# A two-layer decoder step on one core: eighteen entries of a table that delays steps of the woven work

## The chip, the cores and the metric

The kernel runs on one core of a Trainium2 chip. The metric is the device time of one execution in microseconds (us). The core has a matrix engine (PE, with PEld for its weight loads), a vector engine (DVE), a scalar engine (ACT), a general engine (POOL) and a queue that issues the DMAs (SP). Each of them works through its own instructions in the order in which the program gives them; they wait for one another by semaphores. PE writes only to PSUM, which the kernel divides into eight banks.

## The reference

One step of a decoder trunk with two layers, all in f32, for a prompt of 1024 tokens and for eight samples of four tokens each (32 rows). The width is 1024. Each layer computes

```
x <- x + gate(c) * Branch(RMSNorm(x) * (1 + scale(c)) + shift(c))
```

and a last RMSNorm follows. Layer 0's branch is sliding-window attention (16 query heads, 4 key heads of 64, a window of 128, a learned sink); for the samples it reads a cache of 128 keys and values. Layer 1's branch is a gated delta rule (8 key heads, 16 value heads of 128) after a causal convolution over four tokens:

```
def step(S, xs):
    w_v_c, w_k_c, qk_c, q_dec_c, k_dec_c, g_tot_c = xs
    u = w_v_c - w_k_c @ S
    o = q_dec_c @ S + qk_c @ u
    S = S * g_tot_c + k_dec_c.T @ u
```

For the prompt this recurrence runs in chunks, after a triangular solve in each chunk. For the samples each of 8 x 16 states of 128 x 128 is read from memory, used, updated and written back. Both branches end with a SiLU gate and an output projection. Besides the results for prompt and samples the kernel returns the new caches and states.

## The kernel before, in words

**Matrix work.** An f32 operand is split into a high and a low part (`hhi`, `hlo`, `wh`, `wl`), and each product is three matmuls (high by high, low by high, high by low). The bulk of PE's work is such products: the input projections of both layers (`project`, into the tiles `ps_pj`), then the output projections, in `out_block`, a block of 128 rows and two halves of 512 columns at a time. Layer 1 has 18 output blocks: heads 0 to 7 for eight blocks of rows and the samples, then heads 8 to 15 for seven blocks, the samples and the last block.

**The rest is woven in.** Everything else is written as generators, the jobs, which yield a condition wherever they would have to wait. After each matmul of a projection the builder calls `stages()`, which runs every job as far as its conditions let it. `Core.issued` keeps a model of when each engine will be free, so `ready(x)` says whether x should be there by the time at which PE has got, `idle(engine, x)` whether the engine is also free, `soon(x)` the same with some lead, and `bank(tag)` whether a PSUM bank is free; banks of one tag are handed on in turn. All this happens when the program is built: its outcome is the fixed order of the instructions in each engine's queue. `K` and `KR` rank the jobs where several could run.

**The table.** `LATE` (line 271) holds delays. Its key is the job's name, the how-manieth job of that name it is (from 0), and the number of yields that the job has passed. When the condition ahead of that step first holds, the step is held until the model's PE time has advanced by the entry's value, a number in us of that model. `held_off` (line 533) does this and `stages` (line 542) asks it:

```
def held_off(e):
    d = LATE.get((e[2], e[4], e[5]))
    if d is None or plain():
        return False
    if e[6] is None:
        e[6] = nc.free["tensor"]
    return nc.free["tensor"] < e[6] + d

def stages():
    ran = False
    for e in list(jobs):
        while e[0]() and not held_off(e):
            ran = True
            e[0] = next(e[1], None)
            e[5:7] = e[5] + 1, None
...
```

A held step holds back the rest of its own job, and other jobs go ahead of it. It makes no engine wait: an instruction that comes later in its queue still runs as soon as it is at the head and its operands are there. DMAs are the exception in the order: engines get the order of the program, while the DMA queue's order is arranged once more by the framework that places the instructions.

**The jobs that the change touches.**
- `attend_block` (line 1030), 32 of them in layer 0, a row block n for a pair of heads: scores into a bank `lg`, masked row maxima on DVE (`prob`, `mx`), four exponentials on ACT, sums and four scalings on DVE, transposes into banks `mi`, a copy on ACT and one on DVE (`pT`), and for every second block the product with the values into the bank `ob`. Blocks 0 to 15 read the keys of the first head pair; `kproj` (line 916) overwrites them for the second, once block 15 has issued its scores: its `evac` splits the new keys into `khh` (ACT) and `kll` (DVE) and so frees the projection's bank.
- `decayed` (line 2119), one for each key head in layer 1: k.q products for all chunks, eight to a group, multiplied into the decay tiles `DP` on DVE. `chain` (line 2142) is the recurrence over eight chunks; the key projection two heads on waits until a chain is through. `turn` (line 1897) transposes values. `gating` (line 2149) normalizes two chunks' output: sums on ACT, a reciprocal root on POOL, four scalings on ACT, transposes, a multiplication on DVE into `zl`, a store to `gTd`.
- `states_times` (line 2527), the job "states": 64 pieces of the samples' states (tiles `S`, four buffers) are loaded, two at a time multiplied on PE with keys and queries (into the bank `lg`), and the two buffers are loaded anew. It is paced by the progress of the output blocks.
- `core` (line 2580): the samples' recurrence. Its first step closes pools and issues four loads:

```
qk = flat(t2("qk2")).rearrange("p (i h t) -> p i h t", i=2, h=HQ)
nc.sync.dma_start(qk.rearrange("p i h t -> p (i h) t"), smd[0:2 * HQ].rearrange("n p t -> p n t"))
vs = t2("vs")
...
nc.sync.dma_start(gH, gbr[0].rearrange("h (b t) -> (h b) t", t=DS))
nc.sync.dma_start(bH, gbr[1].rearrange("h (b t) -> (h b) t", t=DS))
```

  It starts when chains, outputs and gatings are through (line 2583). Then it transposes on PE into banks `lg`, of which the states' job holds one until its last product, computes decays and 4 x 4 coefficients on DVE, waits for the states (line 2685), forms `VH` (the u), `U` and `oH` (the output) on DVE, and ends with `gsT`. The samples' output blocks (`prepare`, line 2349) wait for the whole core.
- `new_states` (line 2774), the job "new": from the moment the core has `U`, it loads the states once more, multiplies `kb` (ACT) with `U` on PE into banks `mi`, and updates `S` on DVE, two instructions to a product, then stores.
- `gather` (line 2423), one for each half block of the output (36): `y` on DVE from the bank, added to the row block `xt` on POOL (the very last on DVE), then squares on ACT. A gather starts when the one before it has added. `finish` (line 2396) scales a finished block and stores it. `prepare`, odd numbers from 3 on, is `rows_of` (line 2382), the load of a block of rows.

Of the kernel before, what the change touches and what calls it, by code (L numbers as in the profile page):

```python
# [226 lines left out]
def body(tc, I, O, cst_ap, dbg=None):  # L227
# [40 lines left out]
             ("z", 3), ("z", 4), ("z", 5), ("z", 6), ("z", 7)]  # L268
    SE = ("vector", "vector", "vector", "vector")
    LB_, SL = TB  # L270
    LATE = {('ahead', 13, 4): 0.4, ('ahead', 31, 4): 0.8, ('ahead', 57, 2): 0.8, ('attend', 10, 14): 4, ('attend', 12, 32): 1.5, ('attend', 13, 16): 1.5, ('attend', 20, 20): 0.8, ('attend', 22, 17): 0.8, ('attend', 4, 31): 0.4, ('attend', 9, 22): 0.4, ('blocks', 14, 9): 0.4, ('blocks', 5, 4): 0.6, ('blocks', 5, 5): 0.4, ('blocks', 9, 14): 2.5, ('cached', 0, 1): 0.4, ('cached', 1, 4): 0.6, ('cached', 1, 9): 0.4, ('cached', 3, 12): 0.8, ('cached', 3, 18): 0.4, ('cached', 3, 19): 0.8, ('cached', 4, 19): 0.8, ('cached', 4, 8): 2.5, ('chain', 0, 43): 1.3, ('chain', 1, 3): 1.4, ('chain', 2, 3): 2.7, ('chain', 6, 37): 0.4, ('chain', 6, 64): 1.5, ('chain', 7, 13): 0.4, ('chain', 7, 17): 0.4, ('core', 0, 70): 5, ('decay', 1, 6): 4, ('decay', 3, 16): 0.8, ('decayed', 2, 35): 1.5, ('decayed', 4, 25): 0.8, ('decays', 0, 26): 1.5, ('decays', 0, 29): 2.5, ('decays', 0, 43): 1.6, ('gather', 4, 2): 1.5, ('gating', 19, 11): 2.5, ('gating', 6, 11): 0.8, ('gating', 7, 2): 2.5, ('invert', 0, 23): 2.3, ('invert', 2, 22): 4, ('load', 0, 17): 1.5, ('load', 0, 38): 2.5, ('load', 0, 41): 0.4, ('mod', 0, 0): 1.5, ('mods', 0, 60): 2.3, ('mods', 0, 61): 1.5, ('new', 0, 60): 5.2, ('new', 0, 71): 0.7, ('new', 0, 93): 1.4, ('prepare', 0, 3): 3, ('prepare', 0, 8): 0.8, ('prepare', 8, 3): 2.5, ('rows', 0, 2): 1.5, ('samples', 11, 3): 1, ('samples', 18, 3): 1.2, ('samples', 2, 3): 1.5, ('samples', 26, 7): 0.4, ('shape', 7, 12): 0.7, ('shape', 8, 5): 1.5, ('shapes', 0, 21): 4, ('solve', 3, 23): 1.5, ('solve', 3, 7): 0.4, ('split', 0, 3): 0.4, ('split', 0, 6): 2.5, ('split', 3, 1): 1.5, ('squares', 0, 2): 1.5, ('states', 0, 51): 1.5, ('taps', 0, 2): 0.4, ('taps', 3, 2): 4.8, ('taps', 32, 2): 2.5, ('taps', 37, 2): 0.8, ('taps', 4, 2): 4, ('taps', 58, 3): 2.5, ('taps', 6, 3): 1.5, ('taps', 7, 2): 0.8, ('taps', 9, 1): 2.5, ('taps', 94, 2): 0.8, ('turn', 18, 4): 1.7, ('turn', 25, 4): 0.9, ('turn', 26, 4): 2.9}
    XB, FB, ZK, HK0, HK1 = 13, 3, 5, 7, 3

    def psb(tag=None):
# [53 lines left out]
    rows = xp.tile([64, P], F32, name="rows")  # L328
# [84 lines left out]
    def modulation_gate(l, gw, nw, tag):  # L413

        for j in range(2):
            c0 = 2 * D + 512 * j
            nc.sync.dma_start(modGt[32 * j:32 * j + 32], I["b_mod"][l:l + 1, c0:c0 + 512].partition_broadcast(32))
        pg = psb("lg" if l == 0 else "tr")
        wts = {}

        def load(m):

            wts[m] = []
            for k in (2 * m, 2 * m + 1):
                for j in range(2):
                    wt = gw.tile([P, 512], F32, tag=tag, name="wmod", bufs=nw)
                    nc.sync.dma_start(wt, I["w_mod"][l, k * P:(k + 1) * P, 2 * D + j * 512:2 * D + (j + 1) * 512])
                    wts[m].append(wt)

        def step(m):  # L430
            for q, wt in enumerate(wts.pop(m)):
                mm = nc.tensor.matmul(pg[32 * q:32 * q + 32, :], cT[:, 2 * m + q // 2, :], wt, start=(m == 0),
                                      stop=(m == KD // 2 - 1), skip_group_check=True)
            pin[:] = [mm]

        def end():
            nc.vector.tensor_tensor(modGt[0:64], modGt[0:64], pg[0:64, :], ALU.add)
            nc.scalar.copy(modGt[64:P], pg[64:P, :])

        if l == 0:  # L440
            return load, step, end

        def steps():
            load(0)
            for m in range(KD // 2):
                yield lambda: pos[0] >= MS[0] + MS[1] * (2 * m + 1)
                yield ready(*wts[m])
                step(m)
                if m + 1 < KD // 2:
                    load(m + 1)  # L450
            yield soon(pg)
            yield idle("vector", modGt)
            end()

        return steps()
# [77 lines left out]
# [4 lines that stand above are left out]
# [27 lines left out]
    def plain():  # L564
        return not isinstance(nc, Core)
# [311 lines left out]
    if True:  # L877
# [461 lines left out]
        load, step, end = modulation_gate(0, at, 8, "wg")  # L1339
# [441 lines left out]
    if True:  # L1781
# [518 lines left out]
        states = {0: {}}  # L2300
# [571 lines left out]
```

## Time and profile before

| | |
|---|---|
| three runs | 1663.89 us (median), 1662.79 to 1664.79 |
| the profiled execution | 1657.81 us |
| its span, first to last instruction | 1656.0 us |
| PE busy | 1577.5 us of the span |
| DVE, ACT, POOL busy | 1212.5, 871.7, 567.9 us |
| granted PE clock, mean | 0.987 |

The profile is taken from one execution, which has its own time. Rows of the timeline read: start, duration, engine, line, operation, output <- inputs, shapes, how many were merged, and in brackets how long the engine was idle before it and what ended that. Nearly all instructions have line 90, that of the wrapper `Engine` that records them, so a group is known by its tiles. SPq is the DMA queue's issuing, the DMA itself lands later. Names are given without their numbers: `S` stands for `S0` of the states' job, for `S1` of the new states and for the chains' `S`; `qk` for the core's `qk2` too.

### The profile page before, as it was taken

To read this page: it belongs to the slowest core of one execution; us is meant where nothing else is said; L and a number is where in the kernel's file an instruction comes from. 1 tells how busy PE (TensorE), PEld (TensorE's weight loads), DVE (VectorE), ACT (ScalarE), POOL (GpSimd) and SP (SyncE) were. 2 spreads that over 40 slices of the span, in tenths; PEclk is the share of its full clock that TensorE was granted. 3 is DMA by queue.
4 is the path that set the end of the run, shared out by engine and by line. 5 is a ranking of instruction groups with operands and counts; after the bars stand their busy time and mean duration, and the time that the engine had idled before them with its cause. 6 is when DMAs were issued, how large, how long until landed. Compare 5 with 4: busy or idle time off the path is not lost. (4 is left out here: it accounts for less than half of the span.)

```text
span 1656.0 us, 31448 instructions
## 1 busy us (share of the span) xinstructions
PE 1577.5 (95%) x10570; PEld 1333.3 (81%) x10570; DVE 1212.5 (73%) x3535; ACT 871.7 (53%) x2535; POOL 567.9 (34%) x1034
## 2 busy tenths in 40 slices
PE   6999999998999999999899999999999999998996
PEld 5787878887777888889888888988888886676784
DVE  6526767565666679898888778888798876367777
ACT  6535556444345637476473664655656654342332
POOL 1210101112223234363452433545245364333432
PEclk9999999999999999999999999999999999999998
DMA  9642211215344332233322323224132238773976
GB/s 319 184 140 72 67 44 52 65 36 147 115 140 117 94 86 51 69 102 80 99 62 79 89 63 110 54 77 123 47 108 69 57 95 237 232 219 113 281 237 201
DMA packets 286035, 191.76 MB, mean 116 GB/s; under 512 B 98601, under 2 KB 260393, under 8 KB 285842
## 3 DMA queue, kind: packets, MB, share of 16 engines
q1 hardware_dynamic: 285874, 189.75, 40.0%
q8 instruction: 84, 1.38, 0.3%
q14 instruction: 77, 0.63, 0.1%
HBM read 144.68 MB, written 47.04 MB: 116 GB/s over the span
## 5 line engine op out<-in xcount | busy, mean ns | idle before, releaser
L90 PE MATMUL ps_pj<-h2hi,wh 128*128 128x512 f32 (+2 forms) x1128 | 380.7, 337 | 1.4 <-ACT XR L90 1.4
L90 PE MATMUL ps_pj<-h2lo,wh 128*128 128x512 f32 (+2 forms) x1128 | 380.1, 337 | 0.0
L90 PE MATMUL ps_pj<-h2hi,wl 128*128 128x512 f32 (+2 forms) x1128 | 376.8, 334 | 0.0
L90 POOL TENSOR_TENSOR wl<-wr,wh 128x512 fp32r<-128x512 f32 x128 | 172.0, 1345 | 581.7 <-ACT wh L90 559.7
L90 PEld LDWEIGHTS ps_pj<-h2hi,wh 128*128 128x128 f32 x1128 | 213.9, 190 | 17.0 <-ACT XR L90 1.6
L90 PEld LDWEIGHTS ps_pj<-h2hi,wl 128*128 128x128 f32 x1128 | 214.2, 190 | 15.2 <-POOL wl L90 0.6
L90 PEld LDWEIGHTS ps_pj<-h2lo,wh 128*128 128x128 f32 x1128 | 214.2, 190 | 14.5
L90 PE MATMUL ps_pj<-hhi,wh 128*128 128x256 f32 (+2 forms) x376 | 122.4, 329 | 2.5 <-DVE kll L90 1.5
L90 PE MATMUL ps_pj<-hlo,wh 128*128 128x256 f32 (+2 forms) x376 | 122.8, 330 | 0.0
L90 PE MATMUL ps_pj<-hhi,wl 128*128 128x256 f32 (+2 forms) x376 | 121.9, 328 | 0.0
L90 POOL TENSOR_TENSOR xt<-xt,y 128x512 f32<-128x512 f32 (+1 forms) x47 | 63.9, 1365 | 165.4 <-DVE y L90 112.3
L90 DVE SCALAR_TENSOR_TENSOR vT<-XR,cT,vT 128x256 f32<-128x256 f32 (+1 forms) x144 | 85.5, 609 | 29.4 <-ACT vT L90 28.0
L90 DVE TENSOR_TENSOR tmp<-X 64x31 f32<-64x31 f32 (+15 forms) x248 | 95.2, 384 | 10.6 <-POOL X L90 6.9
L90 DVE TENSOR_TENSOR X<-X,tmp 64x31 f32<-64x31 f32 (+15 forms) x248 | 88.4, 356 | 8.5
L90 ACT CAST wh<-wr 128x512 fp32r<-128x512 f32 x128 | 78.6, 615 | 20.0 <-PE ps_pj L90 11.8
L90 PEld LDWEIGHTS ps_pj<-hlo,wh 128*128 128x128 f32 x376 | 70.4, 188 | 13.1 <-issue 8.7
L90 PEld LDWEIGHTS ps_pj<-hhi,wh 128*128 128x128 f32 x376 | 70.3, 188 | 10.6 <-issue 3.1
L90 PEld LDWEIGHTS ps_pj<-hhi,wl 128*128 128x128 f32 x376 | 70.3, 188 | 5.2 <-issue 1.2
L90 ACT ACTIVATE vo<-vo,fo 128x128 f32<-128x128 f32 x128 | 43.0, 393 | 55.1 <-POOL fo L90 55.1
L90 ACT ACTIVATE prob<-prob,nm 128x256 f32<-128x256 f32 (+1 forms) x128 | 62.2, 490 | 18.1 <-DVE nm L90 18.1
L90 POOL TENSOR_TENSOR Xd<-Xc,cst 32x128 f32<-32x128 f32 x128 | 64.4, 503 | 17.7 <-DMA Xc<-Xdd 10.0
L90 ACT ACTIVATE qe<-ps_mi,Eg 128x128 f32<-128x128 f32 x112 | 34.9, 363 | 64.7 <-PE ps_mi L90 64.6
(567 smaller groups left out, 4097.5 us busy)
## 6 DMA issues: line engine op xcount, KB each, us to landing
wr<-in_gdn_w_in SPq DMA_DIRECT2D x96, 256.0 KB
wm<-in_w_mod SPq DMA_DIRECT2D x64, 256.0 KB
S<-in_state_gdn_s SPq DMA_DIRECT2D x38, 256.0 KB
xt<-in_x_prompt SPq DMA_DIRECT2D x16, 512.0 KB
wr<-in_swa_w_in SPq DMA_DIRECT2D x64, 128.0 KB
wmod<-in_w_mod SPq DMA_DIRECT2D x32, 256.0 KB
DP<-gcr SPq DMA_DIRECT2D x64, 128.0 KB
zl<-zd SPq DMA_DIRECT2D x32, 256.0 KB
```

The costliest lines, as they stand in the source:

```text
L90: inst = fn(*args, **kwargs)
```

## The change

One line changes, the table `LATE`. Sixteen entries are new and two are gone; the other entries and all other code stay. Cut to the entries that differ (value in the model's us), with what the step issues:

```
-('attend', 12, 32): 1.5     block 12: second copy of transposed probabilities (DVE)
-('decayed', 4, 25): 0.8     key head 4: a product into DP (DVE)
+('attend', 11, 35): 4       blocks 10 and 11: product with the values (PE)
+('attend', 12, 23): 0.4     block 12: last of four scalings (DVE)
+('attend', 14, 15): 2.5     block 14: first of four exponentials (ACT)
+('attend', 21, 35): 1.5     blocks 20 and 21: product with the values (PE)
+('attend', 23, 13): 0.8     block 23: a masked row maximum (DVE)
+('turn', 31, 4): 2.5        two transposes of values (PE)
+('gating', 31, 6): 2.5      last gating of the last chain: third of four scalings (ACT)
+('core', 0, 1): 4           the core's first step: pools and four loads
+('states', 0, 43): 1.5      a product of two state tiles (PE), two loads
+('states', 0, 47): 1.7      the same, two products later
+('prepare', 9, 1): 4        load of row block 3
+('new', 0, 7): 0.8          an update of a state (DVE)
+('new', 0, 308): 0.8        the same, near the end
+('gather', 13, 2): 1.5      output block 6, second half: y (DVE)
+('gather', 34, 3): 2.5      last output block, first half: addition (POOL)
+('finish', 16, 2): 1.5      samples' rows: first of two scalings (ACT)
```

More of the change, by code (lines that the diff above doesn't have):

```diff
@@ L270, in body @@
     LB_, SL = TB
-    LATE = {('ahead', 13, 4): 0.4, ('ahead', 31, 4): 0.8, ('ahead', 57, 2): 0.8, ('attend', 10, 14): 4, ('attend', 12, 32): 1.5, ('attend', 13, 16): 1.5, ('attend', 20, 20): 0.8, ('attend', 22, 17): 0.8, ('attend', 4, 31): 0.4, ('attend', 9, 22): 0.4, ('blocks', 14, 9): 0.4, ('blocks', 5, 4): 0.6, ('blocks', 5, 5): 0.4, ('blocks', 9, 14): 2.5, ('cached', 0, 1): 0.4, ('cached', 1, 4): 0.6, ('cached', 1, 9): 0.4, ('cached', 3, 12): 0.8, ('cached', 3, 18): 0.4, ('cached', 3, 19): 0.8, ('cached', 4, 19): 0.8, ('cached', 4, 8): 2.5, ('chain', 0, 43): 1.3, ('chain', 1, 3): 1.4, ('chain', 2, 3): 2.7, ('chain', 6, 37): 0.4, ('chain', 6, 64): 1.5, ('chain', 7, 13): 0.4, ('chain', 7, 17): 0.4, ('core', 0, 70): 5, ('decay', 1, 6): 4, ('decay', 3, 16): 0.8, ('decayed', 2, 35): 1.5, ('decayed', 4, 25): 0.8, ('decays', 0, 26): 1.5, ('decays', 0, 29): 2.5, ('decays', 0, 43): 1.6, ('gather', 4, 2): 1.5, ('gating', 19, 11): 2.5, ('gating', 6, 11): 0.8, ('gating', 7, 2): 2.5, ('invert', 0, 23): 2.3, ('invert', 2, 22): 4, ('load', 0, 17): 1.5, ('load', 0, 38): 2.5, ('load', 0, 41): 0.4, ('mod', 0, 0): 1.5, ('mods', 0, 60): 2.3, ('mods', 0, 61): 1.5, ('new', 0, 60): 5.2, ('new', 0, 71): 0.7, ('new', 0, 93): 1.4, ('prepare', 0, 3): 3, ('prepare', 0, 8): 0.8, ('prepare', 8, 3): 2.5, ('rows', 0, 2): 1.5, ('samples', 11, 3): 1, ('samples', 18, 3): 1.2, ('samples', 2, 3): 1.5, ('samples', 26, 7): 0.4, ('shape', 7, 12): 0.7, ('shape', 8, 5): 1.5, ('shapes', 0, 21): 4, ('solve', 3, 23): 1.5, ('solve', 3, 7): 0.4, ('split', 0, 3): 0.4, ('split', 0, 6): 2.5, ('split', 3, 1): 1.5, ('squares', 0, 2): 1.5, ('states', 0, 51): 1.5, ('taps', 0, 2): 0.4, ('taps', 3, 2): 4.8, ('taps', 32, 2): 2.5, ('taps', 37, 2): 0.8, ('taps', 4, 2): 4, ('taps', 58, 3): 2.5, ('taps', 6, 3): 1.5, ('taps', 7, 2): 0.8, ('taps', 9, 1): 2.5, ('taps', 94, 2): 0.8, ('turn', 18, 4): 1.7, ('turn', 25, 4): 0.9, ('turn', 26, 4): 2.9}
@@ new lines, in body @@
+    LATE = {('ahead', 13, 4): 0.4, ('ahead', 31, 4): 0.8, ('ahead', 57, 2): 0.8, ('attend', 10, 14): 4, ('attend', 11, 35): 4, ('attend', 12, 23): 0.4, ('attend', 13, 16): 1.5, ('attend', 14, 15): 2.5, ('attend', 20, 20): 0.8, ('attend', 21, 35): 1.5, ('attend', 22, 17): 0.8, ('attend', 23, 13): 0.8, ('attend', 4, 31): 0.4, ('attend', 9, 22): 0.4, ('blocks', 14, 9): 0.4, ('blocks', 5, 4): 0.6, ('blocks', 5, 5): 0.4, ('blocks', 9, 14): 2.5, ('cached', 0, 1): 0.4, ('cached', 1, 4): 0.6, ('cached', 1, 9): 0.4, ('cached', 3, 12): 0.8, ('cached', 3, 18): 0.4, ('cached', 3, 19): 0.8, ('cached', 4, 19): 0.8, ('cached', 4, 8): 2.5, ('chain', 0, 43): 1.3, ('chain', 1, 3): 1.4, ('chain', 2, 3): 2.7, ('chain', 6, 37): 0.4, ('chain', 6, 64): 1.5, ('chain', 7, 13): 0.4, ('chain', 7, 17): 0.4, ('core', 0, 1): 4, ('core', 0, 70): 5, ('decay', 1, 6): 4, ('decay', 3, 16): 0.8, ('decayed', 2, 35): 1.5, ('decays', 0, 26): 1.5, ('decays', 0, 29): 2.5, ('decays', 0, 43): 1.6, ('finish', 16, 2): 1.5, ('gather', 13, 2): 1.5, ('gather', 34, 3): 2.5, ('gather', 4, 2): 1.5, ('gating', 19, 11): 2.5, ('gating', 31, 6): 2.5, ('gating', 6, 11): 0.8, ('gating', 7, 2): 2.5, ('invert', 0, 23): 2.3, ('invert', 2, 22): 4, ('load', 0, 17): 1.5, ('load', 0, 38): 2.5, ('load', 0, 41): 0.4, ('mod', 0, 0): 1.5, ('mods', 0, 60): 2.3, ('mods', 0, 61): 1.5, ('new', 0, 308): 0.8, ('new', 0, 60): 5.2, ('new', 0, 7): 0.8, ('new', 0, 71): 0.7, ('new', 0, 93): 1.4, ('prepare', 0, 3): 3, ('prepare', 0, 8): 0.8, ('prepare', 8, 3): 2.5, ('prepare', 9, 1): 4, ('rows', 0, 2): 1.5, ('samples', 11, 3): 1, ('samples', 18, 3): 1.2, ('samples', 2, 3): 1.5, ('samples', 26, 7): 0.4, ('shape', 7, 12): 0.7, ('shape', 8, 5): 1.5, ('shapes', 0, 21): 4, ('solve', 3, 23): 1.5, ('solve', 3, 7): 0.4, ('split', 0, 3): 0.4, ('split', 0, 6): 2.5, ('split', 3, 1): 1.5, ('squares', 0, 2): 1.5, ('states', 0, 43): 1.5, ('states', 0, 47): 1.7, ('states', 0, 51): 1.5, ('taps', 0, 2): 0.4, ('taps', 3, 2): 4.8, ('taps', 32, 2): 2.5, ('taps', 37, 2): 0.8, ('taps', 4, 2): 4, ('taps', 58, 3): 2.5, ('taps', 6, 3): 1.5, ('taps', 7, 2): 0.8, ('taps', 9, 1): 2.5, ('taps', 94, 2): 0.8, ('turn', 18, 4): 1.7, ('turn', 25, 4): 0.9, ('turn', 26, 4): 2.9, ('turn', 31, 4): 2.5}
```

## The prediction

> **What bounds the kernel now.** I read the page first, then the busy time by stretch, then PE's waits, and then the timeline of the few places where the eighteen steps run.
>
> ```profile
> span 1656.0 us, 31448 instructions
> PE 1577.5 (95%) x10570; PEld 1333.3 (81%) x10570; DVE 1212.5 (73%) x3535; ACT 871.7 (53%) x2535; POOL 567.9 (34%) x1034
> ```
>
> PE is busy for 1577.5 of 1656.0 us, so 78.5 us are all that any order of the work can win back from idle time, and most of them lie at the start, at the end, or in pieces that this table of delays does not reach. A delay moves an instruction within its engine's queue; it adds no work and removes none. So I look at the places of the edits, and ask where PE stood idle there.
>
> ```profile
> 200.00:300.00 100.00, 97.25 (x673) 79.78 (x672) 69.22 (x247) 55.02 (x182) 13.10 (x10) 1.00 0.22 60
> 215.00:225.00 10.00, 7.76 (x60) 6.12 (x59) 7.66 (x25) 5.73 (x17) 0.00 (x0) 1.00 0.00 1
> 1018.00:1030.00 12.00, 8.83 (x46) 7.26 (x45) 9.68 (x35) 4.98 (x20) 4.59 (x15) 0.86 0.55 128
> 1166.00:1176.00 10.00, 10.00 (x63) 8.83 (x62) 6.98 (x24) 7.83 (x26) 4.89 (x10) 1.00 0.20 53
> 1440.00:1450.00 10.00, 8.89 (x46) 6.49 (x46) 0.69 (x1) 1.03 (x2) 0.00 (x0) 1.00 0.93 236
> 1450.00:1460.00 10.00, 9.65 (x59) 5.31 (x57) 1.97 (x3) 1.36 (x3) 3.80 (x3) 1.00 0.96 280
> 1470.00:1500.00 30.00, 30.00 (x143) 24.94 (x142) 28.58 (x75) 10.95 (x27) 13.93 (x10) 1.00 0.53 171
> 1520.00:1532.00 12.00, 5.40 (x20) 3.47 (x20) 8.63 (x27) 2.50 (x5) 5.46 (x4) 0.72 0.24 87
> 1643.00:1656.00 13.00, 1.55 (x5) 0.74 (x4) 7.67 (x28) 3.99 (x9) 2.54 (x2) 0.66 0.43 132
> ```
>
> Columns: the stretch, its length, busy time of PE, PEld, DVE, ACT and POOL with their instructions, the granted clock, the share of the DMA engines and GB/s. Four stretches lose PE time: 215 to 225 (2.24 us idle), 1018 to 1030 (3.17 us and clock 0.86), 1520 to 1532 (6.60 us and clock 0.72), and the tail after 1643, where DVE is the busiest. At 1166 to 1176 PE loses nothing, and of the 2.75 us that it loses from 200 to 300, 2.24 lie in 215 to 225.
>
> **Part by part. Attention blocks 11 to 14** (steps 11/35, 12/23, 14/15 delayed, 12/32 no longer delayed). PE's two waits here are these, with what ACT and DVE did ahead of the second:
>
> ```profile
> 216.54 0.65 PE L90 MATMUL ps_mi<-cst,prob 128*128 128x128 f32 x4 [0.73 <-ACT pT L90]
> 218.21 0.49 ACT L90 ACTIVATE prob<-prob,nm 128x256 f32<-128x256 f32 x1
> 218.79 1.15 ACT L90 CAST khh<-ps_pj 64x512 fp32r<-64x512 f32 x2
> 224.11 0.40 PE L90 MATMUL ps_pj<-hhi,wh 128*128 128x288 f32 x1 [1.51 <-DVE kll L90]
> ```
>
> The wait of 1.51 us is for the bank that the keys' split (khh on ACT, kll on DVE) frees. That split stands on ACT behind the four exponentials of block 14, of which the last is shown: 4 x 0.49 = 1.96 us. Delaying step 14/15, the first of the four, by 2.5 us puts them behind the split's casts, which then run up to 1.96 us earlier: more than 1.51, so the wait should go. Behind the exponentials wait their sums, scalings and transposes of block 14; they come 2 to 3 us later, under the key projection, which is full PE work. The wait of 0.73 us is for a bank of transposed probabilities; undelayed, the copy 12/32 leaves the pair of banks sooner. The value product 11/35, delayed by 4, holds block 12's transposes until its products are issued; PE has projections to do meanwhile, and 12/23 by 0.4 is one slot. I take -2.0 of the 0.73 + 1.51 = 2.24 us; the ends are -2.24 and +1.5, a wait like the one shown coming back elsewhere.
>
> **Attention 21/35 and 23/13, turn 31/4.** The first two run near 280 us, the third at 1171. All three lie where the rows above leave PE no idle time worth having, and what they hold back, products of an attention pair and two transposes of values that a chain needs far later, is covered by projections. I take 0, from -0.5 to +1.5, since a step that comes too late makes a wait where none was.
>
> **Recurrence: decayed 4/25 loses its delay of 0.8.** In 1018 to 1030 PE waits for the last chunks of chain 3, and no projection may start before it ends.
>
> ```profile
> 1025.82 0.34 DVE L90 SCALAR_TENSOR_TENSOR DP<-ps_lg,sj,DP 128x128 f32<-128x128 f32 x1
> 1027.22 0.61 DVE L90 SCALAR_TENSOR_TENSOR S<-S,Gt,ps_mi 128x128 f32<-128x128 f32 x2 [1.06 <-PE ps_mi L90]
> 1028.75 0.60 DVE L90 SCALAR_TENSOR_TENSOR DP<-ps_lg,sj,DP 128x128 f32<-128x128 f32 x2
> 1029.44 1.06 PE L90 MATMUL ps_lg<-qT,kT 128*128 128x128 f32 x8
> ```
>
> The step is the first of the two DP at 1028.75. Undelayed, both follow the DP at 1025.82, into the 1.06 us in which DVE stands idle before S, and the eight products at 1029.44, which need the bank that they free, come into PE's waits instead of after chain 3. That is worth up to their 1.06 us; if the 0.60 us land before S, they cost that. I take -0.5, between -1.06 and +0.6.
>
> **Samples' core and states, with gating 31/6 and prepare 9/1.** PE's largest loss with a cause near these edits is here:
>
> ```profile
> 1523.16 0.63 PE L90 MATMUL ps_lg<-cst,oH 128*128 128x128 f32 x4 [3.14 <-DVE oH L90]
> 1527.37 0.69 PE L90 MATMUL ps_pj<-h2hi,ohi 128*64 128x512 f32 x1 [3.46 <-DVE ohi L90]
> ```
>
> PE waits 6.60 us until the core's result is there; the output product of the samples is next in its order, and everything after it is shifted by what the core ends later. From 1470 to 1500 DVE is busy for 28.58 of 30 us, so the core cannot shrink there; it can only start its DVE part sooner. That part starts when the last state product is done and its bank is back. In the DMA queue and on PE before that:
>
> ```profile
> 1440.17 1.06 SPq L90 DMA_DIRECT2D gTd<-zl  x1
> 1441.32 1.30 SPq L90 DMA_DIRECT2D S<-in_state_gdn_s  x2
> 1442.96 0.34 SPq L90 DMA_DIRECT2D xt<-x1d  x1
> 1443.71 0.37 SPq L90 DMA_DIRECT2D qk<-smd  x1
> 1444.12 3.41 SPq L90 DMA_DIRECT2D vs<-smd  x1
> 1447.59 1.31 SPq L90 DMA_DIRECT2D gH<-gbr  x1
> 1448.93 0.43 SPq L90 DMA_DIRECT2D bH<-gbr  x1
> 1449.41 0.98 SPq L90 DMA_DIRECT2D S<-in_state_gdn_s  x2
> 1451.59 3.54 SPq L90 DMA_DIRECT2D S<-in_state_gdn_s  x4
> 1448.95 0.60 PE L90 MATMUL ps_lg<-cst,qk 128*32 128x128 f32 x4 [1.11 <-DMA qk<-smd]
> 1458.63 1.35 PE L90 MATMUL ps_lg<-S,zq 128*32 128x256 f32 x8 [0.26 <-DMA S<-in_state_gdn_s]
> ```
>
> The core's first step issues four loads (qk, vs, gH, bH) that hold the queue for 0.37 + 3.41 + 1.31 + 0.43 = 5.52 us; the state tiles behind them come late, and the last state product at 1458.63 waits for one. PE meets the core's first transposes at 1448.95, in front of the state product of step 47, and waits 1.11 us. Delaying the core's first step by 4 us lets the pair of state tiles now at 1449.41 pass the four loads, and lets state products run ahead of the core's transposes. DVE loses little by it: it is busy for 0.69 + 1.97 us in the 20 us up to 1460. The delays of states 43 (1.5) and 47 (1.7) and of the row load (prepare 9/1, 4) work on the same queue; each holds back two loads or one. The gating step 31/6, delayed by 2.5, is the third of four scalings on ACT; behind it are the last scaling, four transposes, zl on DVE and the gTd store at 1440.17, which the core waits for. If the last four state tiles move by the 1.11 us that PE waited and by one issue pair (0.98), the last state product comes 2.1 us sooner. I take -2.0. The bounds: nothing excludes a loss, for 4 + 2.5 = 6.5 us is what the core's start is moved, and a gain ends at the 6.60 us of PE's wait.
>
> The clock adds nothing to this sum. The stretch 1520 to 1532 was granted 0.72 of the clock, so PE also ran slowly after its wait; these rows show a single wait of 2.4 us doing the same:
>
> ```profile
> 552.00:556.80 4.80, 2.43 (x17) 1.95 (x15) 4.49 (x12) 2.69 (x5) 3.81 (x9) 1.00 0.20 56
> 556.90:561.70 4.80, 4.80 (x17) 3.86 (x18) 4.08 (x9) 3.72 (x11) 2.39 (x4) 0.65 0.06 14
> ```
>
> PE was idle for 2.37 us and the next 4.80 us had clock 0.65, a loss of 4.80 x 0.35 = 1.7 us. [...] My sum therefore takes nothing for the clock.
>
> **Around 1523: new 0/7 (0.8) and gather 13/2 (1.5).**
>
> ```profile
> 1525.05 0.98 DVE L90 TENSOR_TENSOR gsT<-gsT,zsm 128x512 f32<-128x512 f32 x1 [0.32 <-ACT gsT L90]
> 1525.96 0.59 DVE L90 SCALAR_TENSOR_TENSOR S<-S,gtb,ps_mi 128x128 f32<-128x128 f32 x2
> ```
>
> The two delayed steps stand ahead of gsT, where DVE is idle for 0.32 us anyway; moved behind, they could add a second pair of 0.59 us ahead of the samples' split, or take this one's place. I take 0, from -0.59 to +0.68.
>
> **Tail: gather 34/3 (2.5), finish 16/2 (1.5), new 0/308 (0.8).**
>
> ```profile
> 1643.91 1.27 POOL L90 TENSOR_TENSOR fng<-fng,y 128x512 f32<-128x512 f32 x1 [3.37 <-DVE y L90]
> 1644.36 0.58 DVE L90 SCALAR_TENSOR_TENSOR S<-S,gtb,ps_mi 128x128 f32<-128x128 f32 x2
> ```
>
> POOL has nothing else to do, so the addition at 1643.91 does not move by itself. But the last half block's multiplication waits for it in the plan, and so falls behind state updates: +0.58 us on the last chain. Against that, the samples' scaling on ACT makes way for the factors of the state products. I take +0.2, from -0.6 to +1.2.
>
> **The sum.** -2.0 - 0.5 - 2.0 + 0.2 = -4.3 us. The profiled execution took 1657.81 us (span 1656.0 and 1.81 around it), 6.08 below the median of the three runs, so I expect it near 1653.5, and the median near 1663.89 - 4.3 = 1659.6.
>
> **Rivals.** *The queue keeps its order* (37%): the core's four loads wait for the gTd store, which gating 31/6 makes later, and the state tiles are still behind them. For it speaks that the queue at 1440.17 and the loads at 1443.71 stand in one chain already. Then the core gives 0, and the rest -2.0 - 0.5 + 0.2 = -2.3 at best; with half of the attention's part, -1.3: about 1662.3.
>
> *The core just comes later* (17%): the two delays add up, 4 + 2.5 us, and the core's start, not the states, decides its end. Its price is PE's wait of 6.60 us grown by as much as the start moves beyond what the states leave free. Against it speaks the row at 1458.63: after its first transposes at 1448.95 the core has nothing to do for some 9 us until the states are done, so up to 9 us of delay are free. It decides from there: if states and core are both late, 6.5 us less the -1.3 of the rest, 5.2 us: 1669.1.
>
> *The delays do nothing*, since a step that isn't ready when its time comes is not delayed further: possible for single entries; it is within the first rival.
>
> **How the numbers follow.** My forecast has 46%: of this, 38 points are faster by more than 0.2% (3.3 us, about what a measurement of this kernel can tell from no change) and 8 within. Its own range, from the bounds of attention and core, is 1654 to 1663. The first rival gives 7 points faster, 28 within, 2 slower; the second 1 within and 16 slower. Together 0.45, 0.37, 0.18. The range for 8 in 10 goes from 1654.5 to 1667, leaving out the worst of the second rival and a core that gains its whole wait.
>
> **What would show it.** The wait for kll near 224 is gone; the DP pair stands before the last S of chain 3; in the queue two more state tiles stand ahead of qk; the last state product comes about 2 us sooner against the output blocks around it, and PE's wait for oH shrinks from 3.14 to about 1 us. I am wrong if the wait for oH and ohi together grows beyond 6.60 us, or if new waits of over 1 us stand in attention after 225, where the held exponentials and products went.

## The result and the profile after

The kernel after takes 1655.34 us (median of 21 runs, 1650.11 to 1661.19), the kernel before, beside it on the same chip, 1663.89 us (21 runs, 1657.51 to 1671.49). The ratio is 0.995, with a 95% interval of 0.9937 to 0.9962: 8.3 us faster, between 6.3 and 10.5. The forecast was 4.3 us, about half of that, with a range that reached to 9.4. The profiled execution has a span of 1648.6 us where that of before had 1656.0.

The page of the kernel after, its span and busy times:

```profile
span 1648.6 us, 31460 instructions
PE 1574.7 (96%) x10570; PEld 1335.4 (81%) x10570; DVE 1211.4 (73%) x3535; ACT 872.1 (53%) x2535; POOL 565.8 (34%) x1034
```

The work is the same. PE's idle time fell from 78.5 to 73.9 us, and its busy time by 2.8 us; where from is seen by stretch. The busy times of the kernel after in stretches that answer to those shown of before, moved by as much as the work had moved (columns as there):

```profile
200.00:300.00 100.00, 99.67 (x700) 83.56 (x699) 70.07 (x250) 57.12 (x185) 13.01 (x10) 1.00 0.22 60
1015.00:1027.00 12.00, 9.80 (x56) 7.53 (x54) 11.64 (x43) 5.80 (x22) 4.15 (x14) 1.00 0.48 116
1437.00:1447.00 10.00, 10.00 (x61) 6.04 (x62) 1.91 (x3) 0.62 (x1) 1.29 (x1) 1.00 1.01 286
1515.00:1527.00 12.00, 6.21 (x23) 3.87 (x23) 8.77 (x31) 2.49 (x5) 5.03 (x4) 0.72 0.21 72
```

From 200 to 300 PE has lost its idle time (2.75 us before, 0.33 now), and 27 more matmuls fit into the 100 us. Around the core's end it is idle for 5.79 us of 12 where it was 6.60, at the same clock of 0.72.

**Attention.** The timeline of ACT and PE in the kernel after, where the wait of 1.51 us was:

```profile
215.61 1.17 ACT L90 CAST khh<-ps_pj 64x512 fp32r<-64x512 f32 x2
219.60 0.51 ACT L90 ACTIVATE prob<-prob,nm 128x256 f32<-128x256 f32 x1
221.18 0.40 PE L90 MATMUL ps_pj<-hhi,wh 128*128 128x288 f32 x1 [0.33 <-DVE kll L90]
```

The key split's casts stand ahead of the exponentials of block 14, and 0.33 us of the wait is left. To measure the whole part I take two places that each kernel has: transposes of `prob` just after 200 us and a single product of scores just after 300 us. Of before, the timeline has

```profile
201.92 1.04 PE L90 MATMUL ps_mi<-cst,prob 128*128 128x128 f32 x8
214.99 0.82 PE L90 MATMUL ps_mi<-cst,prob 128*128 128x128 f32 x4
304.64 0.22 PE L90 MATMUL ps_lg<-khh,qs 128*128 128x128 f32 x1
```

that is 102.72 us between the two places; after has them at 202.01 and 301.06, 99.05 us. The part is worth 3.67 us.

**The samples' core.** The DMA queue of the kernel after, where the state tiles (`S`) were to pass the core's loads:

```profile
1437.92 0.70 SPq L90 DMA_DIRECT2D S<-in_state_gdn_s  x1
1439.45 1.60 SPq L90 DMA_DIRECT2D S<-in_state_gdn_s  x3
1442.89 0.37 SPq L90 DMA_DIRECT2D qk<-smd  x1
```

Four tiles stand ahead of `qk`, where two did. PE's timeline around it, first of before (beside the rows at 1458.63 and 1523.16 shown in the prediction), then of after:

```profile
1441.54 0.64 PE L90 MATMUL ps_lg<-S,zq 128*32 128x256 f32 x8
1460.57 1.04 PE L90 MATMUL ps_lg<-modG,selt 128*32 128x512 f32 x2
1501.77 0.83 PE L90 MATMUL ps_lg<-cst,usH 128*128 128x128 f32 x4 [1.05 <-DVE usH L90]
```

```profile
1438.62 0.64 PE L90 MATMUL ps_lg<-S,zq 128*32 128x256 f32 x8
1455.08 1.39 PE L90 MATMUL ps_lg<-S,zq 128*32 128x256 f32 x8 [0.48 <-DMA S<-in_state_gdn_s]
1457.66 0.60 PE L90 MATMUL ps_lg<-cst,qk 128*32 128x128 f32 x4
1496.95 0.82 PE L90 MATMUL ps_lg<-cst,usH 128*128 128x128 f32 x4 [0.47 <-DVE usH L90]
1518.34 0.63 PE L90 MATMUL ps_lg<-cst,oH 128*128 128x128 f32 x4 [3.14 <-DVE oH L90]
1521.72 0.69 PE L90 MATMUL ps_pj<-h2hi,ohi 128*64 128x512 f32 x1 [2.64 <-DVE ohi L90]
```

The first row of each fence is the same state product, two ahead of anything that the core's entries move; times counted from it compare the kernels without what happened earlier. From there the last state product ends after 1458.63 + 1.35 - 1441.54 = 18.44 us before and 1455.08 + 1.39 - 1438.62 = 17.85 after; the transposes of oH start after 81.62 and 79.72. So the core ends 1.90 us sooner, near the forecast of 2.0, but the last state product comes only 0.59 us sooner, not 2.1. The rest came behind it: the second transposes of `qk` (1461.55 before, 1457.66 after) start 0.97 us sooner, and from there to the transposes of oH 61.61 us became 60.68, the other 0.93. And PE's wait for oH is 3.14 us as before: the gain stands in the small waits ahead of it, that for `qk` (1.11, now none) and that for `usH` (1.05, now 0.47). From the transposes of `usH` to those of oH it is 21.39 us in both. From the transposes of oH to the product that waits for `ohi`, 4.21 us became 3.38.

### The profile page after: what moved, and what is told of

Same layout as the page of the kernel before. It is cut to its first block, busy times and chain, and to the rows that moved or that the text cites. A ratio compares the mean times of both kernels' runs of the same rounds, so it can differ in the third digit from the quotient of the medians.

```text
span 1648.6 us, 31460 instructions
## 1 busy us (share of the span) xinstructions
PE 1574.7 (96%) x10570; PEld 1335.4 (81%) x10570; DVE 1211.4 (73%) x3535; ACT 872.1 (53%) x2535; POOL 565.8 (34%) x1034
## 5 line engine op out<-in xcount | busy, mean ns | idle before, releaser
L90 DVE TENSOR_TENSOR tmp<-X 64x31 f32<-64x31 f32 (+15 forms) x248 | 92.6, 374 | 15.3 <-POOL X L90 11.7
```

The lines of the kernel that those rows point to most:

```text
L90: inst = fn(*args, **kwargs)
```

## The experiments

Each kernel changes only what its diff shows; entries of the table have the values of the change. A single execution is worth little for a time here: over the kernels below the mean granted clock of the profiled execution lay between 0.981 and 0.988, and the 21 runs of the kernel before spread over 14 us. So times are compared by ratios of many runs, and places within a profile by distances from a common row.

### The change in four groups

**Attention alone.**

```
+('attend', 11, 35): 4    +('attend', 12, 23): 0.4  +('attend', 14, 15): 2.5
+('attend', 21, 35): 1.5  +('attend', 23, 13): 0.8  -('attend', 12, 32): 1.5
```

> The kernel before with only the six entries of attention (11/35, 12/23, 14/15, 21/35, 23/13 new, 12/32 gone). Theory, that each group of entries acts where it stands and the groups add up: the layer 0 projections after 300 us come 3.6 us sooner than in the kernel before, as in the kernel after; the waits of 0.73 us for pT and of 1.51 us for kll are gone; from 400 us on nothing changes further, and the time is 3 to 4 us below the kernel before (ratio about 0.998). Rival, that the profiled gain of layer 0 was chance of one execution, and that what counts is the sum of 2.2 us of waits removed: about 2 us (ratio 0.9987). Second rival, that new waits later take it back: ratio 1.000.

Measured: ratio 0.9972 (0.996 to 0.9984). The timeline of PE:

```profile
202.05 1.03 PE L90 MATMUL ps_mi<-cst,prob 128*128 128x128 f32 x8
214.46 1.03 PE L90 MATMUL ps_mi<-cst,prob 128*128 128x128 f32 x8
301.08 0.22 PE L90 MATMUL ps_lg<-khh,qs 128*128 128x128 f32 x1
```

The two places stand 99.03 us apart, 3.69 less than before, the same as with the whole change to 0.02 us. It is no chance of one execution. The waits that went make up 2.42 us of it (PE's busy time from 200 to 300 rose from 97.25 to 99.67). The rest was never idle time on the page: between the two places stand the same 693 matmuls, busy for 99.97 us before and for 98.70 here. Most of that lies in the transposes, whose group over the stretch is 15.3 us busy before and 14.4 here. Those of block 13 stood as rows of 0.82 and 0.65 us with a wait between them, 1.47 us of busy time for what here is one row of 1.03 us. A single transpose lasts 0.27 us on average in both, so the records only overlap less where PE is held up; that `prob` came late is the likely reason, and was not tested by itself.

**The core's group alone.**

```
+('gating', 31, 6): 2.5  +('core', 0, 1): 4     +('states', 0, 43): 1.5
+('states', 0, 47): 1.7  +('prepare', 9, 1): 4
```

> The kernel before with only gating 31/6, core 0/1, states 0/43 and 0/47 and prepare 9/1. Theory, that two pairs of state tiles pass the core's four loads in the DMA queue and the state products end sooner: nothing changes up to 1430 us; four state tiles stand in the queue ahead of qk instead of two; the last state product comes 3 to 4 us sooner, the last output block before 1600 us 2.9 us sooner; ratio about 0.998. Rival, that the core's earlier end in the kernel after came only from the earlier groups (attention and recurrence) and the queue keeps its order: ratio 1.000, the last state product where it was. The rival of the prediction, that the core just comes later: 4 to 6 us slower, ratio 1.003.

Measured: ratio 0.9975 (0.9964 to 0.9986). PE's timeline:

```profile
1445.66 0.64 PE L90 MATMUL ps_lg<-S,zq 128*32 128x256 f32 x8
1462.16 1.37 PE L90 MATMUL ps_lg<-S,zq 128*32 128x256 f32 x8 [0.19 <-DMA S<-in_state_gdn_s]
1525.47 1.08 PE L90 MATMUL ps_lg<-cst,oH 128*128 128x128 f32 x4 [3.14 <-DVE oH L90]
```

The core ends after 79.81 us (before 81.62), the last state product after 17.87 (before 18.44). The group brings the gain by itself, so the rival that the queue keeps its order falls; but the state products were to come 3 to 4 us sooner, and came 0.57. The ratio stands for 4.2 us (2.3 to 6.0), and the place accounts for 1.81 of it; where the rest lies these profiles don't show.

**The recurrence alone.**

```
-('decayed', 4, 25): 0.8  +('turn', 31, 4): 2.5
```

> The kernel before with only decayed 4/25 gone and turn 31/4 new. Theory: the pair into DP moves ahead of the last S of chain 3 and eight lg products into PE's waits, 0.5 us sooner after 1030 us and no more; ratio 0.9997, not told apart from 1. Rival, from the profile after, in which waits of 1.13, 1.14 and 1.14 us stand at 1027, 1081 and 1146: the move makes these waits and the group costs 1 to 3 us; ratio up to 1.002.

Measured: ratio 0.9992 (0.9981 to 1.0003), not told apart from 1. The profile shows a small gain: from the transposes of `vT` at 973.05 to the products of `UZ` at 1263.24 it is 290.19 us before, and here

```profile
978.07 0.66 PE L90 MATMUL ps_tr<-cst,vT 128*128 128x128 f32 x4 [1.14 <-ACT vT L90]
1035.95 1.13 PE L90 MATMUL ps_lg<-Xd,UZ 128*128 128x96 f32 x8 [1.41 <-POOL Xd L90]
1267.92 0.54 PE L90 MATMUL ps_lg<-UZ,M 128*32 128x32 f32 x26 [0.91 <-DVE UZ L90]
```

289.85 us, 0.34 less (0.27 less in the kernel after). DVE's pairs into `DP` went ahead of the last S of chain 3, and PE's wait of 1.14 us for `us` in front of that S is gone, but what followed sooner met a wait for `Xd` that was not there before. The clock moved as well: from 1018 to 1030 us the kernel before was granted 0.86, this one 1.00, and so was the kernel after from 1015 to 1027. What that is worth by itself is not separated: 0.34 us is all that the two places show.

**The late entries alone.**

```
+('new', 0, 7): 0.8      +('new', 0, 308): 0.8   +('gather', 13, 2): 1.5
+('gather', 34, 3): 2.5  +('finish', 16, 2): 1.5
```

> The kernel before with only new 0/7, new 0/308, gather 13/2, gather 34/3 and finish 16/2. The prediction gave this group +0.2 us. The profile after shows the last blocks 1.4 us sooner than the blocks at 1600 us, with the wait for olo at 1.26 us instead of 2.41. Theory from that profile: 1.4 us faster, ratio 0.9992. Rival, that the tail's gain only followed from the earlier core (loads and state updates had more time): 0, ratio 1.000, and the wait for olo still 2.4 us.

Measured: ratio 0.9988 (0.9974 to 1.0002), not settled by the times. What the profile settles is the 0.83 us between oH and `ohi`. POOL and DVE there, first of before (beside the row of gsT at 1525.05 shown in the prediction), then of the kernel after:

```profile
1524.21 2.95 POOL L90 TENSOR_TENSOR xt<-xt,y 128x512 f32<-128x512 f32 x2 [9.97 <-DVE y L90]
1526.47 0.84 DVE L90 TENSOR_TENSOR ohi<-gsT,ohi 128x128 fp32r<-128x128 f32 x1
```

```profile
1519.13 1.27 POOL L90 TENSOR_TENSOR xt<-xt,y 128x512 f32<-128x512 f32 x1 [9.71 <-DVE y L90]
1520.21 0.74 DVE L90 TENSOR_TENSOR gsT<-gsT,zsm 128x512 f32<-128x512 f32 x1 [0.91 <-ACT gsT L90]
1521.39 0.28 DVE L90 TENSOR_TENSOR ohi<-gsT,ohi 128x128 fp32r<-128x128 f32 x1
1521.59 0.68 DVE L90 TENSOR_TENSOR y<-ps_pj,gp 128x512 f32<-128x512 f32 x1
```

One of the two `y` that stood ahead of `gsT` before (a pair of 1.28 us) now stands behind the first split. That does not bring `gsT` sooner: it waits for ACT in both, and starts 1.89 us after the transposes of oH before and 1.87 after. What shrinks is `gsT` itself, from 0.98 to 0.74 us, and the split `ohi`, from 0.84 to 0.28, together 0.80 of the 0.83. Before, POOL adds both `y` in one go until 1527.16, and `ohi` beside it ends at 1527.31; after, POOL has one addition there, until 1520.40, and the next starts at 1522.35, behind `ohi`. The last section has more on this. In this kernel `ohi` takes 0.28 us too; the distance is 3.79 us, although its four transposes took 1.09 us where they took 0.63 in both others, since PE ran at a clock of 0.50 there. For the tail there is no answer: from the product that waits for `ohi` to the end of the span it is 128.6 us before and 126.9 after, but 131.7 in the core's group and 126.4 in the recurrence's, neither of which touches the tail, and 131.0 in this group's own kernel. The wait for `olo` that the expectation went by, 2.41 us before and 1.26 after, is 3.2 here and 0.7 in the recurrence's kernel.

The four ratios multiplied give 0.9927, uncertain by some 0.0024 (the half widths of the four intervals, squared and added; they share their runs of the kernel before, so it is rather more), and the whole change 0.995, by 0.0013. The parts promise some 3.8 us more than the whole gave, which is within these uncertainties: no group is shown to hinder another, and none is shown not to. Attention and the core bring most of it.

### Attention: one step of six

```
+('attend', 14, 15): 2.5
```

> The kernel before with only attend 14/15 new (2.5): the four exponentials of block 14 go behind the key split's casts on ACT. By the prediction: the wait of 1.51 us for kll goes, to 0.3 us or less, the wait of 0.73 us for pT stays, and the projections after 300 us come 1.5 us sooner, not 3.6. Rival, that this step carries the whole of the six entries (also 0.9 us that the transposes of prob waited inside their rows): 3.0 to 3.6 us sooner. Second rival, that without the other entries the held exponentials make a new wait after 225: under 1 us sooner.

A single execution was taken, and its profile. PE's timeline:

```profile
202.84 1.04 PE L90 MATMUL ps_mi<-cst,prob 128*128 128x128 f32 x8
217.45 0.66 PE L90 MATMUL ps_mi<-cst,prob 128*128 128x128 f32 x4 [0.73 <-ACT pT L90]
224.06 0.40 PE L90 MATMUL ps_pj<-hhi,wh 128*128 128x288 f32 x1 [0.57 <-DVE kll L90]
303.79 0.22 PE L90 MATMUL ps_lg<-khh,qs 128*128 128x128 f32 x1
```

100.95 us, 1.77 less than before. The wait for kll went from 1.51 to 0.57, not quite to the 0.3 expected, and that for pT stayed at 0.73: the step does what the prediction said of it. The other 1.9 us belong to the other five entries, which were not run one by one.

### The core: which mechanism

**Half of the group, and the other half.**

```
+('core', 0, 1): 4
```

> The kernel before with only core 0/1 delayed by 4. Theory: this entry alone lets a second pair of state tiles pass the core's four loads in the DMA queue, so it gives what the group of five gave: PE's wait of 1.11 us for qk goes, the last state product and the core's DVE part come 2 us sooner against the output blocks, the blocks at 1500 us 1.8 us sooner than at 1430. Rival, that the group's gain came from the states' and the row load's entries: 0 here. The prediction's rival, that the core just comes later: up to 4 us slower.

```
+('gating', 31, 6): 2.5  +('states', 0, 43): 1.5
+('states', 0, 47): 1.7  +('prepare', 9, 1): 4
```

> The kernel before with only gating 31/6, states 0/43 and 0/47 and prepare 9/1; the core's first step not delayed. The prediction gave these nothing of their own. Theory A, by the prediction: 0 (between -0.3 and +1), the gain belongs to core 0/1. Theory B, that the pairs of state tiles pass the four loads here too, since the gating delayed by 2.5 delays the core's start as well: the same 1.8 to 2 us sooner at 1500 us as the group of five, so that either half does it and the halves don't add up.

Measured: the first step alone 1.0032 (1.0016 to 1.0048), the rest alone 1.0043 (1.0028 to 1.0059). Both halves lose, 5 and 7 us, and together they gain 4. Neither expectation had this.

**The loads on another queue.**

```
-nc.sync.dma_start(flat(vs)..., smd[2 * HQ:2 * HQ + HV]...)      (gH, bH alike)
+inst = nc.nc.scalar.dma_start(dst, src)
+nc.issued("sync", "dma_start", inst.ins, (dst, src), {})
```

> The kernel before, with the core's loads of vs, gH and bH issued from ACT's own DMA queue instead of SP's; the order of PE, DVE and POOL is the same, no delay is changed. Theory, that what the core's four loads cost is the 5.15 us in which they hold the queue ahead of the state tiles: the pair of state tiles issued at 1449.41 goes out 4 to 5 us sooner, the last state product ends 1.5 to 3 us sooner, and the core's DVE part and the blocks at 1520 us come 1 to 2 us sooner; PE's wait of 1.11 us for qk stays, as the order of PE is the same. Rival, that only the order of PE counts (state products ahead of the core's transposes): the last state product comes where it did, 0. Possible cost: the casts ohi on ACT stand behind these issues, up to 3.4 us late.

Measured: 1.0004 (0.9993 to 1.0015).

**The core's start by 12.**

```
+('core', 0, 1): 12
```

> The kernel before with only core 0/1 delayed, by 12 instead of 4, which is more than the 9 us that the prediction called free (from the first transposes of the core at 1448.95 to the last state product at 1458.63). Theory: all state tiles pass the four loads and the last state product comes 3 us sooner still, but the core's transposes then come behind it, and the core's DVE part starts 2 to 6 us later than in the kernel before: slower by 2 to 5 us, ratio 1.001 to 1.003. Rival, that the start of the core is free at any delay and only the states count: faster than with 4.

Measured: 1.0054 (1.0039 to 1.007). For all of these, the places on PE's timeline, counted from the common state product:

| kernel | common product | last state product ends | transposes of oH | to the last | to oH |
|---|---|---|---|---|---|
| before | 1441.54 | 1459.98 | 1523.16 | 18.44 | 81.62 |
| after | 1438.62 | 1456.47 | 1518.34 | 17.85 | 79.72 |
| core's group | 1445.66 | 1463.53 | 1525.47 | 17.87 | 79.81 |
| first step, 4 | 1448.58 | 1466.77 | 1534.77 | 18.19 | 86.19 |
| the rest | 1442.11 | 1465.67 | 1532.78 | 23.56 | 90.67 |
| loads aside | 1446.17 | 1465.06 | 1528.89 | 18.89 | 82.72 |
| first step, 12 | 1447.75 | 1462.84 | 1536.63 | 15.09 | 88.88 |

By the prediction the core's end follows the last state product. It does not: with the delay of 12 that product ends 3.35 us sooner than before, and the core 7.26 us later; with the delay of 4 it ends 0.25 us sooner, and the core 4.57 us later.

The price of the loads needs a second look too. The DMA queue of the kernel with the loads aside:

```profile
1449.01 3.53 SPq L90 DMA_DIRECT2D S<-in_state_gdn_s  x2
```

and ACT's

```profile
1449.80 0.38 ACTq L2605 DMA_DIRECT2D vs<-smd  x1
```

The load of vs, which held SP's queue for 3.41 us, is issued by ACT in 0.38 us, and the pair of state tiles that took its place in SP's queue, 0.98 us before, is now the one that holds it, for 3.53 us. So the hold does not belong to the issue of vs as such. What vs and this pair have in common is the place right behind `qk`, whose load stayed in SP's queue, while the DMA engines are busy all the time (0.93 to 0.96 before, 1.12 here from 1445 to 1465; the view adds up the packets' times, so a share can pass 1). Taking three loads out of the queue brought the last state product nothing: 18.89 us. The queue with the first step delayed by 12 says more:

```profile
1457.63 0.50 SPq L90 DMA_DIRECT2D qk<-smd  x1
1458.18 3.25 SPq L90 DMA_DIRECT2D vs<-smd  x1
```

Eight state tiles stand ahead of `qk` there, where two did; vs is held behind it as before, and the last state product comes 3.35 us sooner. So tiles that pass all four loads do gain, as the prediction had it. Whether it is `qk`'s own transfer that holds what follows, that of vs even from ACT's queue, or any backlog of the DMA engines, was not tested: no kernel moved `qk` alone.

Why the halves lose can be read in a few rows. In the rest alone, PE's timeline has

```profile
1465.05 0.62 PE L90 MATMUL ps_lg<-S,zq 128*32 128x256 f32 x4 [2.90 <-DMA S<-in_state_gdn_s]
```

since two loads of the new states and two transfers of row blocks (x2d, xt) now stand ahead of the last state tile in the queue: the last product ends 5 us later than before, and a delay of that size does move the core. With the first step alone the last product is in time, and the loss comes behind it: from the second transposes of `qk` (1468.58) to those of oH it is 66.19 us, 4.58 more than before, with DVE busy for only 1.56 us more (53.04). ACT there, first of before, then of the first step alone:

```profile
1469.12 0.59 ACT L90 COPY QK<-ps_lg 128x512 f32<-128x512 f32 x1 [0.71 <-PE ps_lg L90]
1470.63 0.62 ACT L90 CAST whB<-wr 128x512 fp32r<-128x512 f32 x1 [0.92 <-DMA wr<-in_gdn_w_out]
```

```profile
1478.79 0.62 ACT L90 CAST whB<-wr 128x512 fp32r<-128x512 f32 x1 [2.77 <-DMA wr<-in_gdn_w_out]
1480.65 0.58 ACT L90 COPY QK<-ps_lg 128x512 f32<-128x512 f32 x1
```

ACT's second copy of QK, which the core's first product `prd` reads, stood ahead of the cast that waits for the last weights (`wr`); now it stands behind two that wait. On DVE four splits of these weights (`wlB`) stand ahead of `prd`, where two do before, and the last of them waits 1.03 us for a cast. So `prd` starts 12.69 us after the second transposes, 9.60 before: 3.09 of the 4.58 us. The order in which DVE and ACT get other jobs' work was chosen anew by the plan, as after any edit.

### What sets the core's end

That gave a second theory: DVE's queue between the last state product and oH. It was tried by taking DVE's six `wlB` splits there away, with every delay and all other orders left alone.

```
-getattr(nc, eng).tensor_sub(lo, raw, f(hi))
+inst = nc.nc.gpsimd.tensor_sub(lo, raw, f(hi))     (where eng is "vector", k from 8 to 12)
+nc.issued("vector", "tensor_sub", inst.ins, (lo, raw, f(hi)), {})
```

> The kernel before, with the six splits wlB of the last weights (0.68 us each on DVE, one of them 1.45 beside POOL, 4.87 us in all) that stand on DVE between the core's second transposes and oH given to POOL. No delay is changed, the order of PE, of ACT and of the rest of DVE is the same. Theory, formed from the profiles of the core's entries: the core's end is set by DVE's queue between the last state product and oH, and every us of other jobs' work that stands there costs one, so the transposes of oH and the blocks after 1530 us come 3.5 to 4.9 us sooner than in the kernel before, ratio 0.997 to 0.998; state tiles, loads and state products stay where they were. Rival, the prediction's, that the last state product's time and the loads set it: 0. Second rival, that DVE's and POOL's work slow each other: half, 2 us.

and in a second kernel with `nc.nc.scalar.copy(lo, raw)` in place of POOL's subtraction, a plain copy that leaves the subtraction out:

> The kernel before with the same six splits wlB taken from DVE, but done as plain copies on ACT (0.6 us each; the subtraction is left out, so this part of the weights' low half is not computed) instead of being given to POOL; POOL's queue stays as it was. Theory: DVE's queue sets the core's end, and the six moved to POOL gained nothing because POOL's instructions hold up DVE's beside them: here POOL has no more to do, so from the second transposes of the core to those of oH it takes 3 to 4.5 us less than the 62.1 us of the kernel before, and the blocks after 1530 us come as much sooner; ratio about 0.998. Rival, that DVE's queue doesn't set the core's end (ACT or PE do): 62 us as before or more, ratio 1.000.

Measured: 1.0001 (0.9989 to 1.0014) with POOL, 0.9984 (0.9969 to 1.0) with ACT. Busy times from the second transposes of `qk` to those of oH, of before, of POOL's kernel and of ACT's:

```profile
1461.55:1523.16 61.61, 57.39 (x274) 45.77 (x274) 51.48 (x137) 24.64 (x50) 19.91 (x14) 1.00 0.50 152
```

```profile
1465.78:1529.48 63.70, 58.24 (x275) 45.62 (x274) 52.68 (x131) 24.54 (x50) 30.07 (x20) 1.00 0.47 146
```

```profile
1466.71:1526.86 60.15, 56.99 (x275) 45.83 (x274) 45.55 (x131) 27.51 (x56) 20.42 (x14) 1.00 0.50 155
```

With POOL's help DVE has six instructions less and is busy for 1.20 us more. The stretch grew by 2.09 us. With ACT's, DVE is busy for 5.93 us less, and the stretch shrinks by 1.46: the sign is the theory's, the size under half of what was expected. PE's wait for `usH` has gone, and DVE now waits 1.41 us for ACT's copy of QK:

```profile
1474.92 0.78 DVE L90 TENSOR_TENSOR prd<-QK 128x512 f32<-128x512 f32 x1 [1.41 <-ACT QK L90]
```

So the theory holds in part. From the transposes of `usH` to those of oH it is 21.39 us before and with POOL's help, 21.17 with ACT's, so DVE's queue counts ahead of `usH` only. And there PE comes next: in ACT's kernel PE is idle for 60.15 - 56.99 = 3.16 us of the stretch, and 3.14 of them are the wait for oH that each of these kernels has; all else is PE's own order of work. The kernels that lose tell the same. In that of the rest and that of the delay of 12 DVE is busy for 50.77 and 51.41 us from the second transposes to oH, no more than before, and the stretch is 2.56 and 5.98 us longer; DVE waits 2.6 and 2.9 us there for ACT's copy of KQ, which are products of PE's; before, it does not wait for that copy.

What POOL did is seen in its own kernel. DVE's timeline and POOL's:

```profile
1471.72 3.72 DVE L90 TENSOR_TENSOR gcH<-gcH,gH 128x1 f32<-128x1 f32 x3
1478.96 1.22 DVE L90 TENSOR_SCALAR rsw<-ssh 128x8 int32<-128x8 int32 x1
```

```profile
1474.14 1.29 POOL L90 TENSOR_TENSOR wlB<-wr,whB 128x512 fp32r<-128x512 f32 x1
1478.86 1.29 POOL L2290 TENSOR_TENSOR wlB<-wr,whB 128x512 fp32r<-128x512 f32 x1
```

Three additions of one element to a partition take 3.72 us (1.94 before, and 0.55 in the kernel with the first step alone, where POOL was idle at that moment), and they end at 1475.44, when POOL's instruction ends (1475.43); the tiny `rsw` takes 1.22 us instead of 0.17 and ends at 1480.18, POOL's at 1480.15.

**The same on the kernel after.**

> The kernel after with the same six splits given to POOL (4.11 us of DVE there). Theory: the blocks after 1530 us come 3 to 4 us sooner than in the kernel after; ratio to the kernel before 0.992 to 0.994, where the kernel after has 0.995. Rival: the tail, which the transfers of the new states fill, gives it back; ratio 0.995.

Measured: 0.9957 (0.9944 to 0.997) against before, so no better than the kernel after with its 0.995. The transposes of oH start 1526.66 - 1443.43 = 83.23 us from the common product, 3.5 later than after. The theory's gain was eaten as in its twin, and the kernel after remains the best version.

## Why the prediction was right, and where it was not

**Sign and range: right; the sum: half of what came.** Faster by more than 0.2% was the likeliest case, and 1655.34 lies within the range, 4.3 us below the forecast. By their places in the profiles the parts give -3.7 for attention, -0.3 for the recurrence, -1.9 for the core and -0.8 behind oH, -6.7 in all, within the interval of 6.3 to 10.5 us.

**Attention, -2.0: mechanism right, size short.** Measured -3.7. The exponentials went behind the casts, and most of the kll wait went, from 1.51 to 0.33 us, in the step named (14/15 alone: -1.77). The term was mis-sized because it was made of PE's idle time alone: that gave 2.4 us, and another 1.3 lay in rows that count as busy, 0.9 of it in the transposes. The new waits of over 1 us after 225, named as a sign of error, did not come up to 300: PE is idle for 0.33 us from 200 to 300 in all.

**Attention 21/35, 23/13 and the turn, 0:** no wait near them in the profile after; not run alone. **Decayed, -0.5:** -0.3 by the profiles, below what the times resolve.

**The samples' core, -2.0: the size right by luck, the steps that carry it wrong.** "If the last four state tiles move by the 1.11 us that PE waited and by one issue pair (0.98), the last state product comes 2.1 us sooner": it came 0.59 us sooner, although the tiles passed the loads, as said. And the link from the last product to the core's end doesn't hold: 3.35 us sooner went with 7.26 us later. "So the core cannot shrink there; it can only start its DVE part sooner" fails too: half of the 1.90 us, 0.93, is a shorter stretch from the second transposes to oH. What the two kernels with the gain have in common, on the timeline, is that the gate's products (`selt`, at 1460.57 before) no longer stand ahead of the core's second transposes, so that these follow the last product after 1.19 us and not 1.57, and that one split `olo` stands ahead of the core's K on DVE, where DVE waits anyway, and no longer behind it; PE's wait for `usH` is 0.58 us shorter. That the move of `olo` is the cause of this last gain was not tested.

**The rivals.** "The queue keeps its order" fell. "The core just comes later" was given up to 9 us of free delay; alone, the delay of 4 costs 5 us already, and that of 12 costs 9. Its price is real, its point of decision was not: by the rows of the losing kernels it is the order of the other jobs' work around the core, which the plan makes anew, and not the slack in the core, as far as they show it. Nothing in the rows of the prediction could have told the halves of the group from the whole. (The first rival's time, with half of attention, is 1663.89 - 1.3 = 1662.6 by its own terms, not 1662.3.)

**oH from 3.14 to 1 us: wrong.** It is 3.14 us after, as before: from `usH` to oH it is 21.39 us in both, so what the core won lay ahead of that and the wait moved along. **Around 1523, 0:** -0.83, more than the bound of -0.59 taken from one pair of S. The term was set at nothing because the rows asked what stands ahead of `gsT`; what counted was how long `gsT` and `ohi` take, and POOL's second addition, which follows the delayed `y`, no longer runs beside them. **Tail, +0.2:** open; the scatter of the tail, 5 us between executions, hides it. **The clock, 0:** right; PE's waits are 3.14 and 2.64 us where they were 3.14 and 3.46, and the stretch still had 0.72, as before: a shorter wait won no clock, just as the single one of 2.37 us from 552 to 556.8 in the kernel before was followed by 0.65. From which wait on the clock drops these runs don't show.

## What to carry to other kernels

Busy time can hide waits: where a group of equal instructions has rows of 0.82 and 0.65 us in one place and one row of 1.03 us in another, look for a wait and put the difference into the sum. A long issue in a DMA queue need not be the price of that transfer: here the hold stayed when vs was moved to another queue, and fell to the transfer that then stood behind `qk` (3.41 us for vs, then 3.53 for a pair of state tiles). And where a planner makes the order, entries don't add up: two halves that cost 5 and 7 us gained 4 us together, so price the order that they end in, and test the group before its parts.

## What the hardware showed that was not expected

Some of DVE's smallest instructions lasted until POOL's beside them ended. In the kernel with the splits on POOL three additions of 128x1 took 3.72 us, 1.2 us each, and a 128x8 operation on integers took 1.22 us, and both rows ended with the POOL instruction beside them to within 0.03 us; in the kernel with the first step alone, with POOL idle beside them, they took 0.55 us (0.18 each) and 0.17. The split `ohi` took 0.84 us beside POOL before and 0.28 after, where POOL was idle. Reductions beside POOL kept their 0.69 us, and so did `y` (0.69 at 1470.94, beside the split on POOL that ends at 1471.69). What held DVE up in the one case and not in the other these runs don't show. The price for this kernel: 4.87 us of DVE's work handed to POOL lengthened DVE's remaining work by 52.68 - (51.48 - 4.87) = 6.07 us.
